# A two-layer hybrid diffusion block on one core: 768 tokens as 384 + 384 instead of 512 + 256

## The chip, the core and the metric

One core of a Trainium2 chip runs one program. The metric is device time in microseconds (us) of one execution; three runs of the kernel before gave a median of 2742.71 us (2742.32 to 2747.55). Engine names: PE (TensorE, the matmul array; its weight loads are shown apart as PEld), DVE (VectorE), ACT (ScalarE), POOL (GpSimd), SP (SyncE, which here only issues DMAs).

## The reference, cut to what matters

The input is 512 latent tokens `x` and 256 context tokens `ctx`, both of width 1024. Two layers each do a token-mixing sub-layer and an MLP:

```python
for l in range(2):
    h  = modulate(rms_norm(x,  g1), sh1,  sc1)      # latents: modulated by c
    hc = modulate(rms_norm(xc, g1), sh1c, sc1c)     # context: modulated by c_ctx
    # one input projection w_in for both: attention q,k,v; GLA q,k,v,gate; low-rank decay; two branch gates
    attn = window_attention(q, k, v, kc, vc, sink)  # blocks of 128; neighbours + all context keys
    o    = bidir_gla(...)                           # gated linear attention, starts from the context's states
    x = x + gt1 * ((sig_a * (attn @ w_branch_attn) + sig_b * (o @ w_branch_gla)) @ w_out)
    x = x + gt2 * (square(relu(modulate(rms_norm(x, g2), sh2, sc2) @ w_ff1)) @ w_ff2)
    # layer 0 does the same for xc with its own modulation; layer 1 needs of xc only keys, values and states
```

So the first layer works on 768 tokens in nearly every product, the second on 512 (and on 768 for keys, values and the GLA keys).

## The kernel before

Activations lie feature-major: features on the 128 partitions, tokens in the free dimension. One buffer of 768 columns holds the latents in columns 0 to 511 and the context in columns 512 to 767. `LAT` and `CTXS` are these two column ranges; six tiles of 128 tokens are numbered 0 to 3 (latents) and 4, 5 (context).

To reach float32 accuracy, each operand is kept as the exact sum of two fp32r parts, and each product is made of three matmuls for each 128 features of depth (`fm`, lines 172 to 174): weight-high by data-high, weight-high by data-low, weight-low by data-high. The weights are the stationary operand, so one matmul streams as many columns as there are tokens in the range: 512 for `LAT`, 256 for `CTXS`. `tm` (lines 184 to 186) makes token-major products, always 256 wide. A weight panel is loaded by SP, its high part made by ACT, its low part by DVE or POOL (`unit`).

A planner orders the instructions of each engine by a simulated time line, starting from the order in which the program emits them; work is thus interleaved across the emitted order. Each engine then runs its queue in order. PSUM banks for products are two called `mm` and, outside attention, one called `mx`; `t2` is a ring of six SBUF buffers for short-lived values.

The stages of the first layer and where the token ranges show:

- `norm(x, t0, n, ...)` normalises and modulates n tokens: four squares on ACT, three adds on DVE, a product with ones on PE, then for each of eight feature tiles one or two DVE operations, one ACT operation and sometimes one on POOL. It is called for at most 256 tokens at a time. A `late` call is emitted only when there is other work ahead of it.
- `keys`: key and value products by tile in the order 4, 5, 0, 1, 2, 3, with `late()` ahead of tile 0: it normalises tokens 256 to 511, tokens 0 to 255 having been normalised before.
- `attention`: blocks `[LAT, CTXS]`, group of heads by group of heads; gates and the branch projection of one block are spread over the steps of the other as PE filler.
- `gla`: low-rank input, decay, GLA queries and keys, gates, and the branch projection, by `LAT` and `CTXS`.
- `merge`: loads the parts of both branches, multiplies, adds and splits them into `Y`, by `LAT` and `CTXS`; the last two gates are made here.
- `project_out`: two parts, `[(512,256), (0,256)]` and `[(256,256)]`; after the first part its tokens are normalised for the MLP.
- `mlp`: eight chunks of 512 hidden features. Chunk 0's first product goes by the three ranges of 256, with `late` ahead of the second; chunks 1 to 7 by `whole = [(0,512), (512,256)]`; the second product by `whole` except in the last chunk, which goes part by part, each part being normalised for layer 1 when it is done (`done`), the last one late, inside `keys`.

In layer 1 the products over the latents are 512 wide; its groups are `[(0,256)]` and `[(256,256)]`.

Of the kernel before, what the change touches and what calls it, by code (L numbers as in the profile page):

```python
# [10 lines left out]
F32 = mybir.dt.float32  # L11
# [29 lines left out]
class Stream:  # L41
    """Columns off..off+T of the residual and of what is made of it."""
# [8 lines left out]


class Pair:
    """A tensor as the exact sum of two float32r parts."""
# [5 lines left out]
class Net:  # L60
# [13 lines left out]
    def shift(self, **bufs):  # L74
        """PSUM for the next phase: tiles by tag."""
# [42 lines left out]
    def wide(self, shape, dt, name):  # L118
        """One of the two places for [128, KD, TOK]."""
# [5 lines left out]
    def mm(self):  # L125
        """A bank for a product; every third one the extra bank if that is free."""
# [13 lines left out]
    def split(self, dst, src, idx, lo_eng=None):  # L140
        """dst.hi[idx] + dst.lo[idx] = src, exactly."""
# [15 lines left out]
    def panel(self, w, c0, rows=(0, D), lo_eng=None):  # L157
        """Columns c0..c0+256 of w: units of 512 rows."""
# [6 lines left out]
    def fm(self, ps, us, f, X, n, t0=0):  # L165
        """ps[:, :n] = (columns f of the units)^T X[.., t0:t0+n]."""
# [9 lines left out]
    def tm(self, ps, us, X, t):  # L176
        """ps = (tokens of tile t of X)^T panel."""
# [11 lines left out]
    def setup(self):  # L189
# [10 lines left out]
        # conditioning: silu of c and c_ctx as columns  # L200
# [13 lines left out]
        # thirty columns of zeros beside the two, so that a product fills its 32 partitions  # L214
# [18 lines left out]
    def layer_small(self, l):  # L233
        """Per-layer vectors as columns, and rows over all partitions."""
# [24 lines left out]
        # all powers of two: the ones' 1 / D is undone, and queries carry the attention scale  # L259
# [7 lines left out]
    def mod_group(self, l, m, bank):  # L267
        """One of the six modulation vectors of a layer, for both streams; summed in a bank or, without one, in SBUF."""
# [33 lines left out]
    def scales(self, x, t0, n):  # L302
        """1 / RMS of tokens t0..t0+n of x, over all partitions."""
# [37 lines left out]
    def attn_consts(self, pool, l):  # L341
        """Masks, and rotary tables with the gains in them."""
# [10 lines left out]
    def qk_norm(self, pool, ps, q, t):  # L353
        """RMS over each head, gain, rotation (latents): [128 tokens, 4 heads, 64]."""
# [744 lines left out]
```

## Time and profile before

| | |
|---|---|
| median of three runs | 2742.71 us |
| profiled execution, first to last instruction (span) | 2738.5 us |
| outside the span, against the median | 4.2 us |
| PE busy | 2612.3 us, 95% |
| DVE busy | 1456.3 us, 53% |
| ACT busy | 1097.8 us, 40% |
| POOL busy | 592.6 us, 22% |
| mean granted PE clock | 0.981 |

The profiled execution's own total is not given apart from its span; the 4.2 us are the difference between the median of the runs and the span. A busy PE is not PE at its peak: the length of a matmul in the trace includes its way through the array, and consecutive ones overlap. The pace is read from the starts: the distance from one start to the next.

### The profile page before, as it was taken

The numbers are of one execution on the slowest core, as the hardware profiler recorded it, in microseconds if no ns is written. First come the engines' busy times: TensorE is split into PE (matmuls) and PEld (weight loads), VectorE is DVE, ScalarE is ACT, GpSimd is POOL, SyncE is SP. The second block draws the span as 40 slices with busy tenths as digits, with TensorE's granted clock in tenths as the row PEclk, the third lists the DMA queues.
The fourth block names the chain that finished last, engine by engine and source line by source line (L and its number), as shares of the span: only waits on it lengthen the run. The fifth ranks groups of instructions, "written<-read, shape, count | busy, mean of one in ns | idle before, by whom it ended". The sixth has DMA issues, their size and how long they took to land. (4 is left out here: it accounts for less than half of the span.)

```text
span 2738.5 us, 41811 instructions
## 1 busy us (share of the span) xinstructions
PE 2612.3 (95%) x16891; PEld 2245.1 (82%) x16891; DVE 1456.3 (53%) x2779; ACT 1097.8 (40%) x2336; POOL 592.6 (22%) x396
## 2 busy tenths in 40 slices
PE   7899999999999899999999998899999998899999
PEld 4788887888888788888887897788788887878888
DVE  4666777534444566333333456777654446643443
ACT  3456554435252334222221244655355434423232
POOL 1313221211120212011111134332122112122122
PEclk7999999999999999999999999999999999999999
DMA  7213123233343533333434241222313325332333
GB/s 246 74 36 72 45 49 103 85 101 93 106 134 93 162 112 94 93 116 116 123 108 126 75 140 49 66 65 60 102 47 93 93 77 174 119 108 89 103 93 101
DMA packets 223830, 269.72 MB, mean 98 GB/s; under 512 B 18480, under 2 KB 185684, under 8 KB 223508
## 3 DMA queue, kind: packets, MB, share of 16 engines
q1 hardware_dynamic: 223636, 267.05, 32.5%
q8 instruction: 132, 2.16, 0.3%
q14 instruction: 62, 0.51, 0.1%
HBM read 244.21 MB, written 22.81 MB: 98 GB/s over the span
## 5 line engine op out<-in xcount | busy, mean ns | idle before, releaser
L97 ACT ACTIVATE whi<-raw 128x1024 fp32r<-128x1024 f32 x322 | 340.1, 1058 | 678.4 <-PE mm L173 270.0
L100 POOL TENSOR_TENSOR wlo<-raw,whi 128x1024 fp32r<-128x1024 f32 x132 | 319.1, 2425 | 926.3 <-ACT whi L97 846.2
L172 PE MATMUL mm<-H,whi 128*128 128x512 f32 (+1 forms) x1168 | 415.6, 356 | 5.8 <-ACT r L97 3.3
L173 PE MATMUL mm<-H,whi 128*128 128x512 f32 (+1 forms) x1168 | 410.8, 352 | 0.8 <-DVE H L337 0.7
L174 PE MATMUL mm<-H,wlo 128*128 128x512 f32 (+1 forms) x1168 | 410.4, 352 | 0.0
L100 DVE TENSOR_TENSOR wlo<-raw,whi 128x1024 fp32r<-128x1024 f32 x190 | 236.8, 1247 | 190.7 <-ACT whi L97 182.7
L172 PEld LDWEIGHTS mm<-H,whi 128*128 128x128 f32 x1168 | 223.2, 191 | 40.6 <-ACT r L97 5.6
L174 PEld LDWEIGHTS mm<-H,wlo 128*128 128x128 f32 x1168 | 222.8, 191 | 28.9 <-issue 0.2
L173 PEld LDWEIGHTS mm<-H,whi 128*128 128x128 f32 x1168 | 222.8, 191 | 28.6 <-DVE H L337 1.0
L103 DVE TENSOR_TENSOR r<-r 128x512 f32<-128x512 f32 (+1 forms) x104 | 89.3, 859 | 253.0 <-ACT hid L97 252.8
L172 PE MATMUL mm<-hid,whi 128*128 128x512 f32 (+1 forms) x552 | 187.8, 345 | 0.0
L173 PE MATMUL mm<-hid,whi 128*128 128x512 f32 (+1 forms) x552 | 186.2, 338 | 1.2 <-DVE hid L100 1.2
L174 PE MATMUL mm<-hid,wlo 128*128 128x512 f32 (+1 forms) x552 | 185.7, 337 | 0.0
L172 PE MATMUL mx<-H,whi 128*128 128x512 f32 (+1 forms) x496 | 171.0, 345 | 3.0 <-DVE sgr L842 2.7
L173 PE MATMUL mx<-H,whi 128*128 128x512 f32 (+1 forms) x496 | 170.2, 343 | 0.0
L174 PE MATMUL mx<-H,wlo 128*128 128x512 f32 (+1 forms) x496 | 168.9, 340 | 0.0
L958 DVE SCALAR_TENSOR_TENSOR x<-mm,mod,x 128x256 f32<-128x256 f32 (+1 forms) x138 | 84.4, 617 | 148.3 <-PE mm L174 148.3
L97 ACT ACTIVATE p<-p,nm 128x512 f32<-128x512 f32 (+1 forms) x128 | 98.1, 768 | 71.3 <-DVE nm L456 71.3
L172 PEld LDWEIGHTS mm<-hid,whi 128*128 128x128 f32 x552 | 104.4, 189 | 23.4 <-issue 8.6
L453 DVE CUSTOM_DVE_ANT_0 p<-S,mask 128x512 f32<-128x512 f32 (+1 forms) x128 | 96.4, 753 | 48.8 <-PE S L451 47.2
L173 PEld LDWEIGHTS mm<-hid,whi 128*128 128x128 f32 x552 | 104.4, 189 | 13.8 <-DVE hid L100 1.4
L174 PEld LDWEIGHTS mm<-hid,wlo 128*128 128x128 f32 x552 | 104.5, 189 | 11.5
(257 smaller groups left out, 6378.1 us busy)
## 6 DMA issues: line engine op xcount, KB each, us to landing
raw<-in_w_ff SPq DMA_DIRECT2D x136, 512.0 KB
raw<-in_w_mod SPq DMA_DIRECT2D x96, 512.0 KB
raw<-in_w_in SPq DMA_DIRECT2D x88, 512.0 KB
raw<-in_w_branch_attn SPq DMA_DIRECT2D x64, 256.0 KB
raw<-in_w_out SPq DMA_DIRECT2D x32, 512.0 KB
raw<-in_w_in SPq DMA_DIRECT2D x32, 256.0 KB
ya<-yd SPq DMA_DIRECT2D x32, 256.0 KB
raw<-in_w_branch_gla SPq DMA_DIRECT2D x16, 512.0 KB
```

What stands on the lines that cost most here:

```text
L97: return self.nc.scalar.activation(out=out, in_=in_, func=func, **kw)
L100: (eng or self.nc.vector).tensor_tensor(out=out, in0=a, in1=b, op=ALU.subtract)
L103: (eng or self.nc.vector).tensor_tensor(out=out, in0=a, in1=b, op=ALU.mult)
L172: nc.tensor.matmul(ps[:, :n], lhsT=wh, rhs=xh, start=(i == 0), stop=False)
L173: nc.tensor.matmul(ps[:, :n], lhsT=wh, rhs=xl, start=False, stop=False)
L174: nc.tensor.matmul(ps[:, :n], lhsT=wl, rhs=xh, start=False, stop=(i == len(ks) - 1))
L453: nc.vector.tensor_tensor_reduce(out=p[:, :nk], in0=S[:, s0:s0 + nk], in1=mask, scale=1.0, scalar=-3e38, op0=ALU.add, op1=ALU.max, accum_o ...
L958: nc.vector.scalar_tensor_tensor(out=xx, in0=ps[:, :n], scalar=self.mod2[:, 5, j, c:c + 1], in1=xx, op0=ALU.mult, op1=ALU.add)
```

## The change

The first layer's 768 columns are cut at 384 instead of 512. `HALVES` holds columns 384 to 767 (latent tile 3 and both context tiles) and columns 0 to 383 (latent tiles 0 to 2), in this order. All feature-major products over 768 tokens, the attention blocks and the parts of `project_out` and `mlp` go by these two; the scan and the read-out of the linear attention keep the split by latents and context (`streams`). Where the modulation differs between latents and context, a range is cut again at column 512 (`pieces`, `onto`, `norms`), so the first half is normalised as 128 + 256 tokens and the second as 256 + 128. `keys` goes by the tiles 4, 5, 3, 0, 1, 2. Layer 1's GLA keys and low-rank input are also made by halves; all else in layer 1 is as before. Comments and docstrings that the diff also removes are left out here.

```diff
+HALVES = [Stream(TOK // 2, TOK // 2, None), Stream(TOK // 2, 0, None)]
+def pieces(t0, n):
+    cut = min(max(SEQ, t0), t0 + n)
+    return [(a, b - a) for a, b in ((t0, cut), (cut, t0 + n)) if b > a]
...
+    def norms(self, x, t0, n, which, H):
+        for a, m in pieces(t0, n):
+            for b in range(a, a + m, 256):
+                self.norm(x, b, min(256, a + m - b), which, H)
...
     def keys(self, pool, H, us, uv, kT, v, late):
-        for t in CTXS.tiles + LAT.tiles:
+        for t in CTXS.tiles + LAT.tiles[-1:] + LAT.tiles[:-1]:
             if t == LAT.tiles[0]:
                 late()
...
+    def onto(self, x, ps, j, t0, n, gates):
+        for a, m in pieces(t0, n):
+            c, xx = int(a >= SEQ), x[:, j, a:a + m]
+            self.nc.vector.scalar_tensor_tensor(out=xx, in0=ps[:, a - t0:a - t0 + m], scalar=gates[:, j, c:c + 1],
+                                                in1=xx, op0=ALU.mult, op1=ALU.add)
     def project_out(self, Y, l, x, groups, done):
...
                     for t0, n in part:
-                        c = int(t0 >= SEQ)
-                        xx = x[:, j, t0:t0 + n]
                         ps = self.mm()
                         self.fm(ps, us, f, Y, n, t0)
-                        nc.vector.scalar_tensor_tensor(out=xx, in0=ps[:, :n], scalar=self.mod[:, 2, j, c:c + 1],
-                                                       in1=xx, op0=ALU.mult, op1=ALU.add)
+                        self.onto(x, ps, j, t0, n, self.mod[:, 2])
...
     def gla_low(self, pool, H, l):
-        for st in (CTXS, LAT):
+        for st in HALVES:
...
     def gla_project(self, pool, H, l, hd, sts):
...
-        for st in (CTXS, LAT):
-            tt = slice(st.off, st.off + st.T)
+        for st in HALVES:
             ps = self.mm()
             self.fm(ps, us, 1, H, st.T, st.off)
-            self.copy(ks[:, tt], ps[:, :st.T], self.either())
+            self.copy(ks[:, st.off:st.off + st.T], ps[:, :st.T], self.either())
             self.tick()
-            if st in sts:
-                ps = self.mm()
-                self.fm(ps, us, 0, H, st.T, st.off)
-                self.act(qs[:, tt], ps[:, :st.T], ACTF.Copy, scale=128.0 ** -0.5)
-                self.tick()
+        for st in sts:
+            ps = self.mm()
+            self.fm(ps, us, 0, H, st.T, st.off)
+            self.act(qs[:, st.off:st.off + st.T], ps[:, :st.T], ACTF.Copy, scale=128.0 ** -0.5)
+            self.tick()
...
-    def gla(self, pool, H, l, E, yb, sts):
+    def gla(self, pool, H, l, E, yb, sts, streams):
...
-            sg = {}
+            sg = [pool.tile([128, width], F32, name="sgr", tag=f"sgr{f}", bufs=1) for f in range(2)]
...
-            blocks = [LAT, CTXS] if CTXS in sts else [Stream(256, 0, 0), Stream(256, 256, 0)]
+            blocks = sts if CTXS in streams else [Stream(256, 0, 0), Stream(256, 256, 0)]
...
-        whole = [(0, SEQ)] + ([(SEQ, CTX)] if width > SEQ else [])
+        whole = [(s.off, s.T) for s in HALVES] if width > SEQ else [(0, SEQ)]
...
     def run(self, es):
-        self.norm(x, 0, 256, 1, H)
-        late = partial(self.norm, x, 256, 256, 1, H)
+        self.norms(x, TOK // 2, SEQ - TOK // 2, 1, H)
+        late = partial(self.norms, x, 0, TOK // 2, 1, H)
         for l in range(DEPTH):
-            sts = [LAT] if last else [LAT, CTXS]
-            groups = [[(0, 256)], [(256, 256)]] if last else [[(SEQ, CTX), (0, 256)], [(256, 256)]]
+            sts, streams = ([LAT], [LAT]) if last else (HALVES, [LAT, CTXS])
+            groups = [[(0, 256)], [(256, 256)]] if last else [[(s.off, s.T)] for s in HALVES]
```

## Rows read from the trace of the kernel before

**Rows 1.** The head of the profile's page: the span, and busy time, share and instructions of each engine with its number of instructions.

```profile
span 2738.5 us, 41811 instructions
PE 2612.3 (95%) x16891; PEld 2245.1 (82%) x16891; DVE 1456.3 (53%) x2779; ACT 1097.8 (40%) x2336; POOL 592.6 (22%) x396
```

**Rows 2.** Busy time by stage; a row is one stretch: its bounds and length in us, busy time of each engine with its instructions, granted PE clock, busy share of the DMA engines, GB/s. In order: keys of layer 0, its attention, its linear attention, its merge and the start of the output projection, the end of its MLP's chunk 0, its MLP's steady part, keys of layer 1, attention of layer 1, the steady part of layer 1's MLP.

```profile
57.00:104.00 47.00, 36.30 (x273) 33.32 (x272) 36.52 (x70) 25.92 (x60) 23.56 (x18) 0.96 0.37 128
104.00:480.00 376.00, 360.69 (x2776) 311.58 (x2776) 256.91 (x687) 198.63 (x541) 82.96 (x54) 0.99 0.22 57
480.00:930.00 450.00, 432.30 (x2743) 370.31 (x2743) 202.77 (x365) 178.84 (x425) 82.97 (x80) 0.99 0.35 106
930.00:1000.00 70.00, 61.90 (x419) 57.25 (x419) 44.87 (x60) 23.49 (x39) 21.09 (x16) 0.93 0.45 140
1058.00:1085.00 27.00, 23.66 (x165) 22.18 (x167) 17.28 (x35) 12.49 (x27) 11.84 (x6) 0.94 0.20 61
1150.00:1560.00 410.00, 410.00 (x2450) 334.02 (x2449) 148.05 (x215) 88.26 (x127) 53.63 (x22) 1.00 0.37 113
1634.00:1690.00 56.00, 46.16 (x348) 42.97 (x348) 47.13 (x84) 30.52 (x68) 25.29 (x19) 0.94 0.31 90
1690.00:1970.00 280.00, 261.34 (x2107) 228.96 (x2106) 201.46 (x525) 151.94 (x377) 77.35 (x46) 0.97 0.26 66
```

**Rows 3.** The time line of PE in the MLP of layer 0: start in us, length in us, engine, line, operation, output and inputs, shape. First the last 256-wide matmuls of a run and the start of a 512-wide run, then the far end of the same run.

```profile
1369.06 0.28 PE L174 MATMUL mm<-H,wlo 128*128 128x256 f32 x1
...
1369.42 0.28 PE L174 MATMUL mm<-H,wlo 128*128 128x256 f32 x1
1369.54 0.40 PE L172 MATMUL mm<-H,whi 128*128 128x512 f32 x1
...
1370.70 0.39 PE L174 MATMUL mm<-H,wlo 128*128 128x512 f32 x1
...
1373.42 0.39 PE L174 MATMUL mm<-H,wlo 128*128 128x512 f32 x1
```

**Rows 4.** The time line of PE in attention of layer 0, four places where two 384-wide score matmuls (one row, x2) stand between other fp32r matmuls; the row behind each tells where they end.

```profile
217.36 0.52 PE L448 MATMUL S<-kT,qT 128*128 128x384 f32 x2
217.72 0.40 PE L451 MATMUL S<-kT,qT 128*128 128x256 f32 x2
229.05 0.51 PE L448 MATMUL S<-kT,qT 128*128 128x384 f32 x2
229.40 0.40 PE L451 MATMUL S<-kT,qT 128*128 128x256 f32 x2
308.17 0.52 PE L448 MATMUL S<-kT,qT 128*128 128x384 f32 x2
308.52 0.40 PE L451 MATMUL S<-kT,qT 128*128 128x256 f32 x2
422.59 0.50 PE L448 MATMUL S<-kT,qT 128*128 128x384 f32 x2
422.93 0.39 PE L451 MATMUL S<-kT,qT 128*128 128x256 f32 x2
```

**Rows 5.** Who PE waited for, by stage: engine, tile and line that waited, who released it, us in total, times, longest. The first two rows are of 930 to 1000 us, the next of 1058 to 1085, the next two of 57 to 104, the next three of 1634 to 1690, the last of 104 to 480.

```profile
PE mm L173 <- DVE Y L100: 7.3, 5, 3.2
PE mx L172 <- ACT sg L97: 0.7, 1, 0.7
PE mm L172 <- ACT r L97: 3.3, 1, 3.3
PE pt L395 <- ACT kd L97: 6.0, 2, 5.8
PE mm L184 <- DVE xn L103: 1.6, 2, 1.3
PE pt L395 <- ACT kd L97: 3.7, 2, 2.4
PE pt L395 <- DVE kd L100: 2.3, 3, 1.1
PE mx L186 <- DVE H L337: 1.3, 1, 1.3
PE S L448 <- DVE rmax L453: 6.7, 8, 2.0
```

**Rows 6.** The late normalisation of tokens 256 to 511 in chunk 0 of layer 0's MLP, DVE's operations of 1049 to 1067 us by kind: line, operation, tiles, shape, number, busy us, mean ns of one, idle time before them and who ended it.

```profile
L330 DVE SCALAR_TENSOR_TENSOR xr<-x,A,rs 128x256 f32<-128x256 f32 x8 | 3.9, 539 | 5.0 <-ACT rs L97 4.3 <-POOL H L100 0.6
L337 DVE SCALAR_TENSOR_TENSOR H<-xr,mod,H 128x256 fp32r<-128x256 f32 x5 | 2.3, 481 | 0.0
L106 DVE TENSOR_TENSOR acc<-acc,sq 128x512 f32<-128x512 f32 x3 | 2.1, 691 | 1.5 <-ACT sq L97 1.4
L332 DVE TENSOR_SCALAR xr<-xr,mod 128x256 f32<-128x256 f32 x3 | 1.0, 347 | 0.0
```

**Rows 7.** The time lines of ACT and DVE around the same call, its first square and its last high and low parts of `H`; and of PE, the last matmul before its wait and the first behind it.

```profile
1049.37 0.62 ACT L97 ACTIVATE acc<-x 128x512 f32<-128x512 f32 x1
1065.42 0.48 DVE L337 SCALAR_TENSOR_TENSOR H<-xr,mod,H 128x256 fp32r<-128x256 f32 x1
1058.27 0.28 PE L174 MATMUL mm<-H,wlo 128*128 128x256 f32 x1
1061.89 0.38 PE L172 MATMUL mm<-H,whi 128*128 128x256 f32 x1 [3.34 <-ACT r L97]
```

**Rows 8.** Groups of DVE instructions of the whole kernel by shape, columns as in rows 6: the same addition to `x` at 512 and at 256 columns, and an addition at 256.

```profile
L958 DVE SCALAR_TENSOR_TENSOR x<-mm,mod,x 128x512 f32<-128x512 f32 x70 | 51.8, 749 | 98.5 <-PE mm L174 98.5
L958 DVE SCALAR_TENSOR_TENSOR x<-mm,mod,x 128x256 f32<-128x256 f32 x68 | 32.7, 482 | 49.8 <-PE mm L174 49.8
L106 DVE TENSOR_TENSOR ya<-mm,ya 128x256 f32<-128x256 f32 x72 | 29.1, 419 | 13.7 <-PE mm L174 13.5
```

More of the change, by code (lines that the diff above doesn't have):

```diff
@@ L805, in gla_read @@
             self.split(G, o, (slice(None), f, slice(st.off, st.off + st.T)), nc.gpsimd)
-    def gla(self, pool, H, l, E, yb, sts):
+    def gla(self, pool, H, l, E, yb, sts, streams):
         nc = self.nc
+        width = sum(st.T for st in sts)
         w = self.io["w_in"][l]
@@ L828, in gla @@
             for st in (CTXS, LAT):
-                S[st], prev = self.gla_scan(st, pool, Eh, ends[st], qs, ks, v, prev, st in sts)
+                S[st], prev = self.gla_scan(st, pool, Eh, ends[st], qs, ks, v, prev, st in streams)
             for _ in fill:
@@ L839, in gla @@
                     self.fm(ps, us, f, H, st.T, st.off)
-                    s = pool.tile([128, st.T], F32, name="sgr", tag=f"sgr{st.col}{f}", bufs=1)
+                    s = sg[f][:, st.off:st.off + st.T]
                     self.sigmoid(s, ps[:, :st.T])
@@ L843, in gla @@
                                                    op0=ALU.mult, op1=ALU.mult)
-                    sg[st, f] = s
-            G = self.pair(pool, [2, sts[-1].off + sts[-1].T], "G")
-            for st in sts:
-                self.gla_read(st, pool, Eh, S[st], v, [sg[st, f] for f in range(2)], G)
+            G = self.pair(pool, [2, width], "G")
+            for st in streams:
+                self.gla_read(st, pool, Eh, S[st], v, [g[:, st.off:st.off + st.T] for g in sg], G)
             for _ in self.gate(H, l, O_SA, 2 * hd, 2, sts, use):
@@ L851, in gla, with mix @@
         return fill
-    def mix(self, l, x, H, us, uv, sts, late):
+    def mix(self, l, x, H, us, uv, sts, streams, late):
         tc, io = self.tc, self.io
@@ L869, in mix @@
             for j in range(KD):
-                n = sts[-1].off + sts[-1].T
+                n = sum(st.T for st in sts)
                 self.nc.sync.dma_start(out=self.yd[:, j, :n], in_=ya[:, j, :n])
@@ L877, in mix @@
                 self.bg = self.mods(0, (2, 3, 4, 5), None)
-            fill = self.gla(pool, H, l, E, yb, sts)
+            fill = self.gla(pool, H, l, E, yb, sts, streams)
             for _ in fill:
@@ L1004, in run @@
             self.load_x(pool, x, LAT, self.io["x"])
-        self.norm(x, 0, 256, 1, H)
-        late = partial(self.norm, x, 256, 256, 1, H)
+        self.norms(x, TOK // 2, SEQ - TOK // 2, 1, H)
+        late = partial(self.norms, x, 0, TOK // 2, 1, H)
         for l in range(DEPTH):
             last = l == DEPTH - 1
-            sts = [LAT] if last else [LAT, CTXS]
-            groups = [[(0, 256)], [(256, 256)]] if last else [[(SEQ, CTX), (0, 256)], [(256, 256)]]
-            yb = self.mix(l, x, H, us, uv, sts, late)
+            sts, streams = ([LAT], [LAT]) if last else (HALVES, [LAT, CTXS])
+            groups = [[(0, 256)], [(256, 256)]] if last else [[(s.off, s.T)] for s in HALVES]
+            yb = self.mix(l, x, H, us, uv, sts, streams, late)
             with tc.tile_pool(name="yp", bufs=1, reuse_waits="tile") as yp:
@@ L1042, in done @@
                             us, uv = [self.panel(self.io["w_in"][l + 1], o) for o in (O_K, O_V)]
-                        late = partial(self.norm, x, t0, n, 1, H)
+                        late = partial(self.norms, x, t0, n, 1, H)
                         if part is groups[0]:
```

9 lines of the change are left out of this document (3 added, 6 removed).

## The prediction

> **What bounds the kernel now.** Read the page's head first: PE is busy 95% of the span and no other engine above 53% [rows 1]. A busy PE proves little, so go to the stages. In the steady part of the first layer's MLP, PE is busy all 410 us at a granted clock of 1.00, with DVE at 36% and ACT at 22% [rows 2]: there the time is the number of matmuls times their pace. In attention DVE is busy 257 of 376 us and PE has short waits for the score maxima. Only at the joints between stages does PE stand: 57 to 104 us and 1634 to 1690 (keys, DVE busy 37 of 47 and 47 of 56), 930 to 1000 (merge, clock 0.93), 1058 to 1085 (late normalisation, clock 0.94). The waits of these joints are small: 7.3 us for `Y` in the merge, 3.3 in the MLP's chunk 0, and in the keys mostly for the last tile's own chain (6.0 and 3.7 for `kd`) [rows 5]. So two questions decide: what 384 columns cost on PE against 512 and 256, and what the new cut does to the joints.
>
> **The pace.** Starts tell it [rows 3]. Three steps of 256-wide matmuls take 1369.42 - 1369.06 = 0.36 us, 120.0 ns each. Twelve steps far inside a 512-wide run take 1373.42 - 1370.70 = 2.72 us, 226.7 ns each. The difference of 106.7 ns for 256 columns is 0.4167 ns a column, and both leave the same constant: 13.3 ns a matmul. On this line a 384-wide one takes 173.3 ns, and two take 346.7 ns, the same as 226.7 + 120.0.
>
> By `fm` and the loops, the products that had two ranges and still have two are, in pairs of matmuls: low-rank input 24, sixteen gates 384, GLA queries and keys 192, GLA gates 192, the two branches 192 each, first MLP product without chunk 0 28 x 24 = 672, second without the last chunk 56 x 12 = 672; together 2520 pairs. On the line they change nothing.
>
> Is 384 on the line? The only 384-wide rows are scores, between other shapes [rows 4]: two of them take 0.36, 0.35, 0.35 and 0.34 us, 175.0 ns each on the mean, with 10 ns of rounding on every start. Bounds, for the 5040 + 768 matmuls that become 384 wide: at 175.0 ns, 5808 x 1.7 = 9.9 us lost; at the smallest, 170 ns, 19 us gained; the largest, 180 ns, would lose 39 us, but a single row carries 5 ns of rounding. I take the line: score matmuls stand just behind a change of width, which costs something itself, as the next term shows.
>
> **Fewer matmuls.** Where three ranges of 256 become two of 384, the columns stay and a constant goes. `project_out` in layer 0: 8 feature tiles x 24 = 192 matmuls fewer. Chunk 0's first product: 4 x 24 = 96. The last chunk's second product: 8 x 12 = 96. Together 384 x 13.3 ns = **5.1 us gained**. The Trainium skill (TensorE: Matmul & The Clock Gate, section Back-to-back issue gap) gives a constant of about 2.5 ns at full clock instead; by it these 384 would save 1.0 us and the sum below would be 2737 us. The trace disagrees with it here, 13.3 ns at both widths, and I go by the trace.
>
> **No change of width.** The first five steps of a 512-wide run behind a 256-wide one take 1370.70 - 1369.54 = 1.16 us, 232 ns each, 27 ns more in all than five later ones [rows 3]. The first layer has 181 products of 512 columns by the loops (1 + 16 + 8 + 8 + 32 + 32 + 28 + 56), each at most once behind a narrower one: 181 x 27 = 4.8 us at the most. The planner puts some 512-wide ones behind each other, so I take **3.5 us gained**; zero if equal widths have a start-up of their own.
>
> **The merge.** The first part of `project_out` now needs only columns 384 to 767 of `Y`, and three open banks hold 3 x 24 x 173.3 = 12.5 us of work instead of 3 x 24 x 120 = 8.6. PE can go on for 3.8 us more before it depends on the last of `Y`. It waits 7.3 us there and the clock falls to 0.93 over 70 us, about 5 us lost [rows 2, 5]. DVE's work there stays (two 384-wide operations for 512 + 256). I take **3 us gained**; bounds 0 and 12.
>
> **The normalisations.** Three sets of 768 tokens (for attention in layer 0, for its MLP, for layer 1) become 128 + 256 and 256 + 128 instead of three of 256. DVE spends 3.9 + 2.3 + 2.1 + 1.0 = 9.3 us on one of 256 [rows 6]. One of 128 is not in the trace: halving an operation from 512 to 256 columns takes it from 749 to 482 ns [rows 8], so 267 ns go and 128 columns should take about 348, 0.72 of 256; the three adds fall from 691 to 419. That is (3.9 + 2.3 + 1.0) x 0.72 + 1.3 = 6.5 us. A set costs 2 x 9.3 + 2 x 6.5 - 3 x 9.3 = 3.7 us of DVE more. What lies around each set:
>
> In `keys` of layer 0 DVE is nearly the bound, and the first latent tile needed is now tile 3, whose input comes in last: **2 us lost**, bounds 0 and 6. In chunk 0 of the MLP the first half is normalised behind 8 x 24 x 173.3 = 33 us of PE work instead of 23, but the late half is 384 tokens behind 4 x 24 x 173.3 = 16.6 us instead of 256 tokens behind 23.0: **1 us lost**, bounds 3 gained (the wait of rows 5 gone) and 13 lost (rival below). In `keys` of layer 1 the same shift happens; the first half is normalised behind 8 x 12 x 173.3 = 16.6 us instead of 11.5, the late one behind three tiles instead of four: **1 us gained**, bounds 4 and -6.
>
> **The rest costs nothing, by this cover.** The addition to `x` is cut once more (128 + 256 and 384 for 512 + 256): about 0.2 us more on DVE, 8 x 7 times, 12 us in an MLP where DVE is idle 64% [rows 2]; without that cover it would be those 12 us. Panels, their high and low parts and the weight DMAs stay in number. The context's scan needs the first half's GLA keys alone, which still come first. Transfers of `yd` and `gd` change only in width, 384 instead of 512 and 256. In attention the latent steps had (12288 + 18432) / 8 = 3840 columns of filler each and the context steps 24576 / 4 = 6144; now the first block's six steps have 6144 and the second's six have 3072, 30720 over the eight latent steps either way. The score waits are 6.7 us in all [rows 5], so I put this at nothing, within 4 us either way.
>
> **The sum.** -5.1 - 3.5 - 3 + 2 + 1 - 1 = -9.6 us. The profiled span of 2738.5 becomes 2728.9; with the 4.2 us by which the median lies above that span, the forecast is **2733 us**. One run of this kernel can be told from no change at about 0.2%, 5.5 us.
>
> **Rivals.**
> A: the 384-wide matmul has the pace of the score rows, 175.0 ns. Then 9.9 us come back and the time is 2743 us: no change. For it: these are the only rows of that width. Against it: their neighbours differ in width, and both known widths lie on one line.
> B, slower: the late normalisation outgrows its cover. In chunk 0 the late 256 tokens took from 1049.37 to 1065.90, 16.5 us, and PE, with 23.0 us of cover, still waited 3.3 [rows 5, 7]: the call started about 9.8 us into the cover. If it starts as late again and 6.5 us for 128 tokens come behind, 9.8 + 16.5 + 6.5 - 16.6 = 16.2 us of wait, 13 more than now. With half as much in each of the two keys stages, 26 us are lost against 9.6 gained: 2759 us. It decides from 15 us of added wait on. For it: the call is still emitted behind the first half's products, and `t2` has six buffers. Against it: before, the start was late because the preceding normalisation was itself squeezed into 23 us of PE work; it now has 33.
> C: the joints gain more: the merge's wait and its low clock go wholly (12 us instead of 3) and the keys of layer 1 gain 4: 2721 us. For it: the first part needs half of `Y`. Against it: DVE makes `Y` feature tile by feature tile, so the last tile is late for both halves.
>
> **Chances.** The forecast, 2727 to 2737: 0.43. A and what else ends within 5.5 us of no change: 0.26. B: 0.18. C: 0.13. Faster by over 0.2% is the forecast and C, 0.56; the same 0.26; slower 0.18. The range goes from C's time to short of B's full price, 2721 to 2753 us.
>
> **What would show it.** PE should have 384 fewer fp32r matmuls, about 16,500 in all; 384-wide starts 173 ns apart with no start-up of a run; in the MLP's steady part the same length as before, less about 2 us; the wait for `Y` in the merge under 5 us; the waits for `H` behind chunk 0's first half and behind tile 3 of the keys under 5 us each. A pace of 175 ns or more, or waits for `H` of 10 us and more at any of the three normalisations, would make the forecast wrong.

## The result and the profile after

The changed kernel takes 2780.8 us (median of four runs, 2774.1 to 2785.1) beside 2742.5 us of the kernel before on the same chip (2741.9 to 2747.6): ratio 1.013, interval 1.0116 to 1.0145. It is 38 us slower; 2733 us were forecast, 2721 to 2753. Its profiled run has a span of 2781.8 us, 43.3 more than [rows 1].

The head of the page after:

```profile
span 2781.8 us, 41265 instructions
PE 2615.1 (94%) x16519; PEld 2348.2 (84%) x16519; DVE 1471.9 (53%) x2884; ACT 1108.3 (40%) x2370; POOL 591.0 (21%) x405
```

PE has 372 matmul records fewer than in [rows 1] (384 by the loops; a few records can be missing) and is no longer busy for it: the 43 us are idle time and low clock (PE is idle 166.7 us of the span, before 126.2). Where? Cut both traces at the first matmul of each stage (first key product, first query product, first product with the decay's inputs, first `Y`, last `Y`, first `hid`, last `hid` of the layer, and so on):

| stage, length in us | before | after | difference |
|---|---|---|---|
| keys of layer 0 | 61.2 | 71.3 | +10.0 |
| attention, then GLA and merge of layer 0 | 378.7, 468.8 | 381.2, 469.7 | +2.4, +0.9 |
| output projection of layer 0 | 84.2 | 76.2 | -8.0 |
| chunk 0 of layer 0's MLP, up to its second product | 41.3 | 53.9 | +12.6 |
| rest of that MLP | 555.9 | 552.2 | -3.7 |
| keys of layer 1 | 55.4 | 68.7 | +13.2 |
| attention, GLA and merge of layer 1 | 619.2 | 632.7 | +13.5 |
| output projection and MLP of layer 1 | 53.3, 369.7 | 54.1, 369.9 | +0.8, +0.2 |

(1.2 us more lie ahead of the first key product; parts carry one rounding.) So four stages lose 49 us and two gain 12. Busy time by stage after, columns as in [rows 2]: keys of layer 0, its output projection, chunk 0, the rest of the MLP, keys of layer 1, its attention and GLA; and the 22 us in the middle of chunk 0 alone.

```profile
44.70:116.00 71.30, 53.24 (x371) 47.82 (x369) 53.85 (x111) 38.26 (x92) 27.69 (x24) 0.88 0.40 132
966.90:1043.10 76.20, 71.22 (x394) 68.87 (x393) 59.02 (x97) 34.86 (x61) 18.87 (x15) 0.98 0.44 138
1043.10:1097.00 53.90, 38.67 (x211) 36.62 (x210) 28.18 (x55) 22.07 (x46) 12.80 (x10) 0.84 0.16 49
1097.00:1649.20 552.20, 552.20 (x3276) 510.03 (x3274) 215.58 (x372) 131.25 (x199) 83.33 (x37) 1.00 0.35 109
1649.20:1717.90 68.70, 51.84 (x351) 48.40 (x349) 47.21 (x94) 32.43 (x75) 25.90 (x21) 0.84 0.25 78
1717.90:2350.60 632.70, 599.48 (x3963) 526.69 (x3961) 374.14 (x807) 307.28 (x711) 146.19 (x106) 0.98 0.28 81
1060.00:1082.00 22.00, 6.77 (x27) 4.96 (x27) 14.87 (x39) 11.60 (x29) 5.32 (x5) 0.61 0.07 24
```

The rest of the MLP is pure PE, 552.20 of 552.20 us at a clock of 1.00. Chunk 0 and both keys stages have PE idle a quarter of the time, and the clock falls with it. In the 22 us of the last row no engine is full: PE 6.8, DVE 14.9, ACT 11.6. That is a chain of waits, not an engine at its limit.

What the chain is shows the time line of ACT and DVE in chunk 0 (start, length, what; in brackets the engine's idle time before it): the last addition to the late half's `x`, the relus of the first half's four products, the first squares of the two pieces of the late normalisation, the second piece's logarithm, and the last operation on ACT.

```profile
1043.44 0.62 DVE L627 SCALAR_TENSOR_TENSOR x<-mm,mod,x 128x384 f32<-128x384 f32 x1
...
1048.53 0.49 ACT L105 ACTIVATE r<-mm 128x384 f32<-128x384 f32 x1 [4.20 <-PE mm L182]
1051.76 0.49 ACT L105 ACTIVATE r<-mx 128x384 f32<-128x384 f32 x1 [2.18 <-PE mx L182]
1055.92 0.49 ACT L105 ACTIVATE r<-mm 128x384 f32<-128x384 f32 x1 [3.11 <-PE mm L182]
1060.09 0.49 ACT L105 ACTIVATE r<-mm 128x384 f32<-128x384 f32 x1 [3.11 <-PE mm L182]
1060.47 0.62 ACT L105 ACTIVATE acc<-x 128x512 f32<-128x512 f32 x1
...
1070.79 0.42 ACT L105 ACTIVATE acc<-x 128x256 f32<-128x256 f32 x1 [0.37 <-DVE H L350]
...
1077.09 0.37 ACT L105 ACTIVATE rs<-pt,eps 128x128 f32<-128x128 f32 x1 [2.12 <-PE pt L322]
...
1082.16 0.29 ACT L105 ACTIVATE H<-xr 128x128 fp32r<-128x128 f32 x1
```

`x` is complete at 1044.06 us. ACT idles 12.6 us in four gaps until 1060, but the first square comes at 1060.47, directly behind the fourth relu: the call stands behind the first half's four products in emitted order, and so in ACT's queue. From there the chain of both pieces takes until 1082.45, 22.0 us. (DVE ends its last operation 0.2 us later.) The second piece's squares (1070.79) come only when the first piece is largely applied: the first two of them wait for operations on `H`, which by the code free the six buffers of `t2`. PE's waits in chunk 0 (who waited, for whom: us in all, times, longest):

```profile
PE pt L322 <- DVE acc L114: 13.6, 2, 9.9
PE mx L180 <- ACT H L105: 1.6, 1, 1.6
```

The first row is PE in front of the matmuls with ones of the two pieces, waiting for sums of squares. In the two keys stages the same two kinds appear smaller, and behind them a wait for the last keys, the first row of layer 0, the second of layer 1 (before: 6.0 and 3.7, [rows 5]):

```profile
PE pt L408 <- ACT kd L105: 9.4, 2, 5.9
...
PE pt L408 <- ACT kd L105: 7.7, 2, 7.3
```

The GLA of layer 1 is another matter. Its code for the 512-wide latents is untouched, yet it has waits that the kernel before does not have there (before, nothing at all for `sgr`, `a` or `st`):

```profile
PE mx L180 <- DVE sgr L859: 4.0, 3, 3.5
PE pt L809 <- DVE a L805: 2.2, 2, 1.2
PE pt L809 <- DVE st L768: 2.0, 1, 2.0
```

The first is a wait for the extra bank `mx`; that the other two follow from it is tested below. `mm()` gives every third product this bank by a counter. The first layer calls it 20 times less (8 in `project_out`, 4 in chunk 0, 8 in the last chunk), so the counter stands at 523 instead of 543 when layer 1's GLA heads start: remainder 1 instead of 0. From there on both kernels call it equally often, so all heads keep the shift.

Two theories share the 38 us, then, each with a rival. **O, the order**: the late normalisation is emitted behind all the work that could hide it. Its rival **A, the amount**: 384 tokens in two pieces are longer than 16.6 us of products wherever they start. And **P, the phase** of the bank counter, against the rival that the GLA only inherits what came before it.

### The profile page after: what moved, and what is told of

Same layout as the page of the kernel before. It is cut to its first block, busy times and chain, and to the rows that moved or that the text cites. A ratio compares the mean times of both kernels' runs of the same rounds, so it can differ in the third digit from the quotient of the medians.

```text
span 2781.8 us, 41265 instructions
## 1 busy us (share of the span) xinstructions
PE 2615.1 (94%) x16519; PEld 2348.2 (84%) x16519; DVE 1471.9 (53%) x2884; ACT 1108.3 (40%) x2370; POOL 591.0 (21%) x405
## 5 line engine op out<-in xcount | busy, mean ns | idle before, releaser
L180 PE MATMUL mm<-H,whi 128*128 128x384 f32 (+2 forms) x1072 | 378.5, 354 | 3.2 <-DVE sgr L859 3.2
L181 PE MATMUL mm<-H,whi 128*128 128x384 f32 (+2 forms) x1072 | 375.6, 350 | 0.0
L182 PE MATMUL mm<-H,wlo 128*128 128x384 f32 (+2 forms) x1072 | 374.7, 350 | 0.1
L180 PE MATMUL mx<-H,whi 128*128 128x384 f32 (+2 forms) x560 | 198.0, 354 | 8.9 <-DVE sgr L859 5.0
L180 PE MATMUL mm<-hid,whi 128*128 128x384 f32 (+2 forms) x564 | 197.9, 356 | 0.1
L181 PE MATMUL mm<-hid,whi 128*128 128x384 f32 (+2 forms) x564 | 194.9, 348 | 3.0 <-DVE hid L108 3.0
L181 PE MATMUL mx<-H,whi 128*128 128x384 f32 (+2 forms) x560 | 196.5, 351 | 0.8 <-DVE H L350 0.7
L182 PE MATMUL mx<-H,wlo 128*128 128x384 f32 (+2 forms) x560 | 196.4, 351 | 0.0
L182 PE MATMUL mm<-hid,wlo 128*128 128x384 f32 (+2 forms) x564 | 194.7, 348 | 0.0
L627 DVE SCALAR_TENSOR_TENSOR x<-mm,mod,x 128x256 f32<-128x256 f32 (+3 forms) x210 | 107.9, 537 | 157.9 <-PE mm L182 157.9
L180 PEld LDWEIGHTS mx<-H,whi 128*128 128x128 f32 x560 | 106.5, 190 | 19.0 <-DVE sgr L859 6.4
L192 PE MATMUL mm<-whi,H 128*128 128x256 f32 x384 | 112.5, 294 | 7.6 <-ACT H L105 6.3
L498 PE MATMUL pt<-pT,v 128*64 128x128 f32 x1280 | 105.4, 287 | 9.7 <-DVE pT L120 6.3
```

The lines of the kernel that those rows point to most:

```text
L180: nc.tensor.matmul(ps[:, :n], lhsT=wh, rhs=xh, start=(i == 0), stop=False)
L181: nc.tensor.matmul(ps[:, :n], lhsT=wh, rhs=xl, start=False, stop=False)
L182: nc.tensor.matmul(ps[:, :n], lhsT=wl, rhs=xh, start=False, stop=(i == len(ks) - 1))
L192: nc.tensor.matmul(ps, lhsT=xh, rhs=u.hi[:, k], start=(i == 0), stop=False)
L498: nc.tensor.matmul(po[h * 64:(h + 1) * 64, 0:128], lhsT=v[:, keys[i + a], g * HD:(g + 1) * HD], rhs=pT[:, (2 * a + h) * 128:(2 * a + h + 1 ...
L627: self.nc.vector.scalar_tensor_tensor(out=xx, in0=ps[:, a - t0:a - t0 + m], scalar=gates[:, j, c:c + 1], in1=xx, op0=ALU.mult, op1=ALU.add)
```

## The experiments

Lengths by stage in us, from the profiled run of each (single executions; most runs of one kernel lie within 5 us of their median, single ones 9 off it, so a microsecond or two of a stage says little; the run of e6 in the table is the longest of its ten, that of e1 the shortest of its four).

| | before | after | e1 | e2 | e3 | e6 | e8 | e11 | e13 | e14 |
|---|---|---|---|---|---|---|---|---|---|---|
| keys 0 | 61.2 | 71.3 | 67.4 | 70.6 | 61.2 | 67.2 | 65.3 | 63.7 | 66.6 | 70.4 |
| projection 0 | 84.2 | 76.2 | 76.2 | 75.8 | 80.8 | 76.3 | 75.9 | 75.6 | 75.8 | 75.7 |
| chunk 0 | 41.3 | 53.9 | 46.3 | 54.0 | 41.4 | 46.9 | 50.4 | 39.7 | 49.8 | 46.2 |
| rest of MLP 0 | 555.9 | 552.2 | 552.2 | 552.2 | 554.1 | 552.2 | 552.2 | 553.1 | 553.1 | 553.1 |
| keys 1 | 55.4 | 68.7 | 57.5 | 67.3 | 54.5 | 56.2 | 63.6 | 51.9 | 59.0 | 59.3 |
| attention, GLA 1 | 619.2 | 632.7 | 633.2 | 620.8 | 620.7 | 625.5 | 620.9 | 619.3 | 632.5 | 635.7 |
| MLP 1 | 369.7 | 369.9 | 370.0 | 370.1 | 372.7 | 361.0 | 364.6 | 363.4 | 369.8 | 365.4 |

### Is it the joints or the steady parts? (e3)

From the changed kernel, only the joints are put back:

```diff
-        for t in CTXS.tiles + LAT.tiles[-1:] + LAT.tiles[:-1]:
+        for t in CTXS.tiles + LAT.tiles:
...
-        self.norms(x, TOK // 2, SEQ - TOK // 2, 1, H)
-        late = partial(self.norms, x, 0, TOK // 2, 1, H)
+        self.norm(x, 0, 256, 1, H)
+        late = partial(self.norm, x, 256, 256, 1, H)
...
-            groups = [[(0, 256)], [(256, 256)]] if last else [[(s.off, s.T)] for s in HALVES]
+            groups = [[(0, 256)], [(256, 256)]] if last else [[(SEQ, CTX), (0, 256)], [(256, 256)]]
```

> The changed kernel, with 384 + 384 kept in the products of the steady parts (low-rank input, gates, GLA queries and keys, branches, MLP's first product without chunk 0 by its own order of parts) and in the attention blocks, but the joints as before: project_out, chunk 0 and the last chunk in three parts of 256, normalisations of 256, keys in the old order. Theories O and A alike: the whole loss lies in the joints (and the phase of the extra bank, which is the old one here): 2739 us, the kernel before less some 3.5 us for products that no longer change width. Rival W: the two parts of 384 cost in the steady products or the attention blocks themselves: 2755 us or more.

Measured: 2741.7 us, the kernel before beside it 2745.4; ratio 0.9991, interval 0.9981 to 1.0001. The whole loss is in the joints and the phase; rival W falls. What 384 + 384 brings in the steady parts alone cannot be told from nothing by the total; the rest of the MLP shows 1.8 us. There PE never waits and the length hardly scatters: 552.2 us in after, e1, e2, e6 and e8, 555.9 or 556.0 in before, e7, e9, e10 and e12.

### The late call first (e1)

In `keys` of both layers and in chunk 0 of layer 0's MLP:

```diff
-            if t == LAT.tiles[0]:
+            if t == CTXS.tiles[0]:
                 late()
...
-                        if (t0, n) == halves[1]:
+                        if (t0, n) == halves[0 if width > SEQ else 1]:
                             late()
```

> The changed kernel (2780.8 us) with the late half's normalisation emitted ahead of the first half's products instead of behind the available ones: in keys of both layers at the first tile instead of the fourth, in chunk 0 of layer 0's MLP ahead of both halves. All work stays. Theory O (order): in the changed kernel the late squares stand in ACT's queue behind the four relus of the first half though x is ready 16 us earlier, and PE then waits. About 25 us come back: 8 of the 10 us that keys of layer 0 lost, 10 of 12.6 in chunk 0, 8 of 13 in keys of layer 1: 2756 us, and PE waits of 10.4 us (chunk 0) and 7.5 us (keys of layer 1) shrink under 3 us. Rival A (amount): 384 tokens in two pieces are too much DVE and ACT work for this cover wherever they start, since the first half's chain then waits for the late one: under 6 us come back, 2775 us or more.

Measured: 2761.8 us, ratio 1.0065 (1.0049 to 1.0082); 18 to 19 us come back, half of the loss. By stage 7.6 in chunk 0, 11.2 in keys of layer 1, but 3.9 of 10 in keys of layer 0. The order counts, and it is not all: chunk 0 keeps 5 us. PE's waits in chunk 0 now:

```profile
PE pt L322 <- DVE acc L114: 4.3, 1, 4.3
PE mm L180 <- ACT r L105: 3.9, 1, 3.9
```

The relus now stand behind the normalisation in ACT's queue. Three products of the first half run and fill the three open banks; PE stands at the second piece's matmul with ones, and then the fourth product waits on for a bank, until the first relu behind the normalisation frees one:

```profile
1056.95 0.49 ACT L105 ACTIVATE r<-mm 128x384 f32<-128x384 f32 x1 [0.21 <-DVE H L350]
```
```profile
1057.50 0.69 PE L180 MATMUL mm<-H,whi 128*128 128x384 f32 x1 [3.94 <-ACT r L105]
```

The stage of layer 1's attention and GLA stays long (633.2 us), so its loss does not come in with the late normalisation. (The 10.4 us of the expectation are 9.9 in the trace.)

### The phase of the extra bank (e2, e9)

Both add one statement at the start of the heads; e2 to the changed kernel, e9, with `(1 - self.turn) % 3`, to the kernel before:

```diff
         ga = self.gla_low(pool, H, l)
+        if l == 1:
+            self.turn += -self.turn % 3
```

> The changed kernel with one more line: at the start of layer 1's GLA heads the turn that sends every third product to the extra PSUM bank is brought to a multiple of three, as it stands there in the kernel before (543; in the changed kernel 523). Layer 1's GLA is 13 us longer in the changed kernel though its code is the same. Theory P (phase): the gate product now lies in the extra bank that the decay also wants, and the bank waits for VectorE's multiply; 8 to 13 us come back, 2768 to 2773 us. Rival: the loss comes in with what enters the stage (the late norm, the order of loads); nothing comes back, within 3 us of 2780.8.

> The kernel before with the turn brought to one modulo three at the start of layer 1's GLA heads, where the changed kernel has it; nothing of the change itself. Theory P: the phase alone costs it 8 to 13 us in layer 1's GLA, 2753 to 2758 us, with waits of the extra bank for VectorE's multiply with the gate. Rival: the phase only hurts together with the 384-wide low-rank input and keys of the changed kernel; the same as before.

Measured: e2 2769.1 us, ratio 1.0091 (1.0076 to 1.0107) where the changed kernel had 1.013, 11 to 12 us less, nearly all of it in layer 1's attention and GLA (620.8, before 619.2). e9 2755.5 us, ratio 1.0037 (1.0025 to 1.0050), 10.8 us more than before; its attention and GLA of layer 1 are 12.6 us longer, and it has the same waits as the changed kernel:

```profile
PE mx L172 <- DVE sgr L844: 4.1, 3, 3.5
PE pt L793 <- DVE st L752: 2.2, 1, 2.2
PE pt L793 <- DVE a L789: 2.1, 2, 1.2
```

P is shown from both sides: taken out of the changed kernel, all but 1.6 us of this stage's loss and all three waits go; put alone into the kernel before, they come. In the trace of the changed kernel one of these waits can be followed: a gate's product lies in `mx`, the next head's key product takes `mx` too, and starts at 2162.62 us, behind DVE's multiply of the gate:

```profile
2161.82 0.75 DVE L859 SCALAR_TENSOR_TENSOR sgr<-mx,lcol,sgr 128x512 f32<-128x512 f32 x1 [0.79 <-ACT sgr L105]
```
```profile
2162.62 0.44 PE L180 MATMUL mx<-H,whi 128*128 128x384 f32 x1 [3.45 <-DVE sgr L859]
```

### Both corrections (e6)

e1 and e2 together, the late call first also in layer 1's chunk 0 (`halves[0]` in both layers).

> The changed kernel with both corrections, the late normalisation ahead everywhere (also in chunk 0 of layer 1's MLP, where PE waits 7 us in both kernels) and the turn at a multiple of three at layer 1's GLA. O and P: 25 + 10 us come back and 4 more in layer 1's MLP: about 2742 us, the kernel before. If O or P falls, 2755 us or more.

Measured: 2736.1 us, ratio 0.9966 (0.9954 to 0.9978): faster than the kernel before, and 6 us better than expected. Layer 1's MLP gives 8.9 us instead of 4; the other joints are as in e1. Layer 1's attention and GLA show 625.5 us in this longest of its runs, e2 620.8. 5.6 us in chunk 0 and 6 in keys of layer 0 stay.

### What is left: PE's queue, or the length? (e8, e13, e14)

e8 is e6 with the late call one product group later: `t == CTXS.tiles[1]` in keys, between the two panels of the first half in chunk 0.

> The changed kernel with the turn set as in the run with both corrections, but the late normalisation emitted one product group later: in keys behind the first tile, in chunk 0 behind the first two of four products. Ahead of everything, its matmul with ones stands before the first half's products in PE's queue, and PE waited 4.6 + 4.3 us for it at the start of chunk 0 and 3.3 us in keys of layer 0 with products ready behind it. Theory Q (what is left of the loss in the joints is PE's own queue): those waits go, 5 us back in chunk 0 and 3 in keys of layer 0 against the run with both corrections, 2728 us. Rival A (what is left is the amount of 384 tokens in two pieces): the waits only move, 2734 us or more.

Measured: 2750.1 us, ratio 1.0018 (1.0008 to 1.0027), 14 us worse than e6. Theory Q falls. Chunk 0 grows by 3.5 us and keys of layer 1 by 7.4. In chunk 0 PE now waits once, longer:

```profile
PE pt L322 <- DVE acc L114: 8.9, 1, 8.9
```

It is the second piece's matmul with ones, but nothing that was ready stands behind it: the four products of the first half are through at 1052, and the next product needs the late half's `H`. The chain only starts later than in e6, behind the second relu and 9.1 us into the stage:

```profile
1043.69 0.62 ACT L105 ACTIVATE acc<-x 128x512 f32<-128x512 f32 x1
```

Nor was PE's queue what e6 lost in chunk 0: it has the same two waits as e1 (4.3 us for the sums, 3.9 for a relu), and the second, for the relu's bank, would have held the fourth product without the first. So the call in one piece keeps the relus waiting if it is emitted first, and starts late if it is emitted later.

So the call was cut in two emitted steps: `stat` (squares and additions of both pieces) and the rest (ones, logarithm, application). e13 emits both at the old place, so that the second piece's squares no longer follow the first piece's application; e14 emits `stat` first and the rest at the old place. In e13, e14 and e11 the first half's two pieces, normalised for layer 1 in the last chunk, get the new order too.

```diff
+    def two(self, x, t0, n, which, H):
+        cut = [(b, min(256, a + m - b)) for a, m in pieces(t0, n) for b in range(a, a + m, 256)]
+        accs = [self.stat(x, b, m) for b, m in cut]
+        yield
+        for (b, m), acc in zip(cut, accs):
+            self.norm(x, b, m, which, H, self.rms(acc, m))
```

> The changed kernel with one edit: where the late normalisation stands, the squares and additions of both pieces come ahead of the first piece's application. In the changed kernel the second piece's squares wait for buffers of the first's application, and its matmul with ones keeps PE 10.4 us in chunk 0. Theory S: the 22.0 us from the first square to the last H become about 17: 5 us back in chunk 0 and 3 in each of the two keys stages, 2770 us against 2781. Rival: ACT and VectorE are busy through the 22 us and only the order within changes: within 3 us of the changed kernel.

> The changed kernel with one edit: the squares and additions of both late pieces are emitted ahead of the first half's products, the matmuls with ones and the application stay behind them, where they were. Theory S: the statistics (8.7 us in chunk 0 for the first piece, and the second piece's) leave the exposed stretch; of 22.0 us about 13 stay: 9 us back in chunk 0, 5 in keys of layer 0, 6 in keys of layer 1, 2761 us. Rival: the exposed stretch is set by the application alone: under 4 us back in all, 2777 us.

Measured: e13 2762.4 us, ratio 1.0066 (1.005 to 1.0082), 18 us back with the order of a few ACT and DVE instructions alone; 4.1 in chunk 0 where 5 were expected, 4.7 in keys of layer 0 and 9.7 in keys of layer 1 where 3 each were. How much of the 9.7 comes from the first half's new order was not told apart. The time line of ACT in its chunk 0:

```profile
1052.04 0.62 ACT L105 ACTIVATE acc<-x 128x512 f32<-128x512 f32 x1
1052.56 1.66 ACT L105 ACTIVATE sq<-x 128x512 f32<-128x512 f32 x3
1054.12 0.40 ACT L105 ACTIVATE acc<-x 128x256 f32<-128x256 f32 x1
...
1069.58 0.40 ACT L105 ACTIVATE H<-xr,mod 128x128 fp32r<-128x128 f32 x1 [0.72 <-DVE xr L357]
```

The chain takes 1069.98 - 1052.04 = 17.9 us instead of 22.0. e14: 2759.9 us, ratio 1.0055 (1.0037 to 1.0073). Chunk 0 gives 7.7 us, keys of layer 1 9.4, keys of layer 0 only 0.9 of the 5 expected; against e13 it wins 3.6 us in chunk 0 and 4.4 in layer 1's MLP and loses 3.8 in keys of layer 0. Its only wait in chunk 0 is for the application:

```profile
PE mx L180 <- ACT H L105: 7.7, 1, 7.7
```

### Statistics first, the rest behind one product (e11, e12)

e11 is the changed kernel with the phase of e2, `stat` ahead of the first product and the rest behind the first of four products (keys: behind the first tile). e12 is the kernel before with the same two steps, its late part one piece.

```diff
+                    late = late()
+                    next(late)
                     for t0, n in halves:
-                        if (t0, n) == halves[1]:
-                            late()
...
                                 ff1(us[p], p, f, t0, n)
+                                list(late)
```

> The changed kernel with the turn at a multiple of three and the normalisation in two emitted steps: the squares and additions of both late pieces ahead of the first product, the rest (matmul with ones, logarithm, application) behind the first of the four products in chunk 0 and behind the first tile in keys. So ACT's squares stand ahead of the relus, and PE has work in front of the matmuls with ones. Theory S (three queues in series: the squares behind relus on ACT, the second piece's squares behind the first piece's application by the buffers of t2, the matmuls with ones ahead of ready products on PE): chunk 0 takes 43 us (run with both corrections: 46.9), keys of layer 0 64 (67.2), keys of layer 1 55 (56.2): 2728 us, faster than before. Rival L (length: 384 tokens in two pieces take 22 us from the first square to the last H, against 16.6 us of products, whatever the order): 2735 us or more, the run with both corrections.

> The kernel before with the same two steps at the same places; its late part is one piece of 256. Theory S: the squares no longer stand behind relus and PE has work ahead of the ones: chunk 0 of layer 0 within 2 us of 41, chunk 0 of layer 1 8 us shorter, keys the same within 2 us: 2736 us. Beside the run of the changed kernel in this form it tells what the change is worth when neither waits in a queue: 8 us less for the changed one by the terms that held; within 4 us if the 384-token normalisation eats them.

Measured: e11 2729.4 us, ratio 0.9936 (0.9915 to 0.9957), 15 us faster than the kernel before. Chunk 0 takes 39.7 us, less than before (41.3), keys of layer 1 51.9 (55.4), keys of layer 0 63.7 (61.2). L, the length, falls. S holds for the two queues on ACT (squares behind relus, second piece behind first); that the matmuls with ones held up ready products in chunk 0 no run shows. The time line of ACT in its chunk 0: the second piece's squares, the first relu behind them, the two logarithms, the next relu.

```profile
1041.59 1.02 ACT L105 ACTIVATE sq<-x 128x256 f32<-128x256 f32 x3
1044.46 0.49 ACT L105 ACTIVATE r<-mm 128x384 f32<-128x384 f32 x1 [1.86 <-PE mm L182]
...
1047.24 0.47 ACT L105 ACTIVATE rs<-pt,eps 128x256 f32<-128x256 f32 x1 [1.72 <-PE pt L329]
...
1052.07 0.37 ACT L105 ACTIVATE rs<-pt,eps 128x128 f32<-128x128 f32 x1 [0.43 <-DVE H L364]
...
1059.41 0.49 ACT L105 ACTIVATE r<-mx 128x384 f32<-128x384 f32 x1
```

All squares end at 1042.6, two microseconds ahead of the first relu. The second relu waits until 1059.41 behind the application, but PE goes on: three open banks take three products of 384 columns, 3 x 24 x 173.3 = 12.5 us, and it waits once:

```profile
PE mx L180 <- ACT r L105: 2.5, 1, 2.5
```

e12: 2747.0 us, ratio 1.0012 (1.0003 to 1.0022); 2736 was expected. Layer 1's MLP gives 7.7 us back as expected, but chunk 0 of layer 0 takes 46.5 us (41.3) and keys of layer 1 57.9 (55.4). In its chunk 0 the relus stand behind the application as in e11, but here three banks hold only 3 x 24 x 120.0 = 8.6 us of 256-wide products:

```profile
PE mm L172 <- ACT r L97: 7.2, 2, 5.0
```

What the change is worth with this order is therefore not 8 but 18 us (2747.0 - 2729.4). That part of it is the order, which suits two wide parts better than three narrow ones, is a reading of these waits (7.2 us for relus against 2.5), not a run of its own.

### The late call moved in the kernel before (e7, e10)

e7 has e6's places in the kernel before, e10 those of e8, both without the split.

> The kernel before with the late normalisation emitted ahead of the first product, in keys and in chunk 0 of both layers' MLPs. Here the late part is 256 tokens in one piece, with more product work behind it in the first layer. Theory O: the old place costs the old kernel too, but only where two equal parts remain, as in layer 1's MLP: 8 us back there, as the changed kernel with the same edit showed, and up to 3.5 in chunk 0 of layer 0 (its wait there); keys stay within 3 us. About 2733 us, 0.996 of before. Rival: the order matters only for 384 tokens; the same as before within 0.2%.

> The kernel before with the late normalisation emitted behind the first tile in keys and behind the first two products in chunk 0 of both layers. Beside the changed kernel with the same place it tells what the change itself is worth once the order is right in both: by the terms that held (384 fewer matmuls 5.1 us, no change of width 3.5, the joint of the projection 8, less one more piece of normalisation) the changed one should be 6 to 12 us shorter. If the change is worth nothing once the order is right, the two are within 4 us. This kernel itself: 2732 us, no more than 3 us from the one with the late normalisation first.

Measured: e7 2748.5 us, ratio 1.0009 (0.9998 to 1.0020); e10 2745.6 us, ratio 1.0003 (0.9991 to 1.0015). Both as before, where 2732 to 2733 were expected. e7's layer 1 MLP is 8.6 us shorter (361.1), but its chunk 0 in layer 0 takes 48.2 us (41.3) and its keys of layer 1 60.1 (55.4): what one joint gains, the others lose. So the place of the call in the kernel before was no plain flaw; with three parts of 256 it fits. Against e10, e8 is 4 us longer, not 6 to 12 shorter: with the call in one piece in the middle the change costs 4 us. With the call first it is worth 12: e6 at 0.9966 of before against e7 at 1.0009.

## Why the prediction was wrong, step by step

**The pace: right.** The time line of PE in the MLP of layer 0 after, twenty-one steps of 384-wide matmuls apart:

```profile
1375.84 0.33 PE L182 MATMUL mm<-H,wlo 128*128 128x384 f32 x1
...
1379.48 0.33 PE L182 MATMUL mm<-H,wlo 128*128 128x384 f32 x1
```

3.64 / 21 = 173.3 ns, the 173.3 that were read off the line; rival A's 175.0 is out. At 0.4167 ns a column (granted clock 1.00, the level of 2.4 GHz) 384 columns take 160 ns, so the constant is again 13.3 ns. The Trainium skill's 2.5 ns, given for an isolated matmul (TensorE: Matmul & The Clock Gate, section Back-to-back issue gap), does not hold for these products at any of the three widths.

**Fewer matmuls, no change of width: right where PE never waits.** In the rest of layer 0's MLP 96 matmuls fewer are 1.3 us and 84 products without a change of width 84 x 27 = 2.3 us at the most, 3.6 together; the stage is 3.7 us shorter. e3, which keeps the 96, shows 1.8. In attention and GLA of layer 0 nothing of it is seen. Over all profiled runs GLA there is rather some 2.6 us longer with halves (nine runs, 467.9 to 472.4, mean 470.0) than with latents and context (five runs, 466.2 to 468.9, mean 467.4), and attention 1.4 (379.9 and 378.5 in the mean); why stays open.

**The merge: right, a little small.** The projection's stage is 8.0 us shorter; 192 matmuls are 2.6 of it, so 5.4 come from the wait and the clock, for which 3 were taken. The clock of the stage is 0.98, and the wait for `Y` is 3.8 us in all instead of 7.3.

**The late normalisation in chunk 0: this step failed.** The sum had +1; it is +12.6, nearly 14 with the 1.3 us of matmuls saved. The sum of the sizes came out: 16.5 + 6.5 = 23 us were worked out for 384 tokens, 22.0 came, and the cover was 16.6 us, the four products, as given. That is in part luck: the 256 tokens took 14 us, not 16.5 (in these ACT stood 4.8 for the matmul with ones, which came behind products on PE), and the 128 added 8, not 6.5. What was wrong is the start. The prediction let the call start early in its cover, because "before, the start was late because the preceding normalisation was itself squeezed". But [rows 7] already had the first square at 1049.37 us, and what stood directly ahead of it on ACT, in the kernel before, was the fourth relu of the first part:

```profile
1049.09 0.38 ACT L97 ACTIVATE r<-mm 128x256 f32<-128x256 f32 x1 [1.50 <-PE mm L174]
```

The call waited for its place in the queue. With three parts, four products were still to come behind that place; with two parts, none. It started 17.4 us into the stage (1060.47 against 1043.1), when the cover was used up. Rival B had the mechanism, and still took the start at 9.8 us, 7.6 too early. It had worked the 9.8 out from PE's wait of 3.3 us as if that were for `H`; [rows 7] shows it ended by a relu, and from the stage's start the call began 12.9 us in (1049.37 against 1036.5). Nor is the wait after the one for `H` that was named as a sign: PE stands 13.6 us for the sums of squares and 1.6 for `H`.

**Keys of both layers: the same step failed.** +2 and -1 were taken; +10.0 and +13.2 came. Order alone (e1, e13) gives back 3.9 and 4.7 us in layer 0 and 11.2 and 9.7 in layer 1; the new order of tiles was not tried by itself. The sum of these three stages' misses, 8.0 + 11.6 + 14.2, is 34 us.

**The phase of the bank counter: not seen at all.** "The rest costs nothing" went through panels, DMAs, scans and fillers, but not through a counter that runs on over both layers; this term stood at nothing without a reason. It costs 11 to 12 us in a stage whose 512-wide code was not changed.

These two are nearly the whole miss: 34 + 12 = 46 us of the 48 between forecast and result.

**How far the amount counts.** O alone was too simple as well. e1 and e6 leave 5 us in chunk 0 although the call starts as early as it can, and e7 and e8 show that an earlier or a later place can lose. What e11 shows is that the normalisation is not too long (39.7 us, under the kernel before) once its statistics stand ahead of the first product and the rest behind one product. Open is what still makes keys of layer 0 2.5 us longer than before in e11.

## What to carry to other kernels

When a change makes the parts of a loop fewer and wider, look at each call that is emitted between two parts: its cover is what stands behind it, and its start is its place in each engine's queue, read from the instruction directly ahead of its first one, not from when its data were ready. A call that uses several engines in turn takes a place in each of their queues; here it was worth more to emit its statistics ahead of the first product and the rest behind one product than to move it whole. And a counter that deals out banks over the whole program is part of the change: twenty products fewer here shifted which product met which bank two stages later.

## What the runs showed of the hardware that was not expected

A wait cost more than its own length. In the 22 us of chunk 0 in which PE was busy for 6.8, the mean granted clock was 0.61. From 1075 to 1079 us it was 0.50, the level of 1.2 GHz, after PE had idled 9.9 us; the 384-wide products behind the waits start 0.32 us apart instead of 0.173:

```profile
1080.55 0.53 PE L181 MATMUL mm<-H,whi 128*128 128x384 f32 x1
1080.87 0.53 PE L182 MATMUL mm<-H,wlo 128*128 128x384 f32 x1
1081.19 0.53 PE L181 MATMUL mm<-H,whi 128*128 128x384 f32 x1
```

From 1082.6 us to the end of the stage the clock is 1.00 again. In chunk 0 this is little: PE is busy for 38.7 us, before for 38.1 with 1.3 us more of matmuls, so some 2 of the 12.6 us, an estimate from the busy times. In keys of layer 1 it is more: PE is busy 51.8 us for 351 matmuls at a clock of 0.84, where the kernel before needs 45.6 for 347, some 6 of the 13.2 us. That stage in the kernel before, and then chunk 0 in e11, with all but 2.5 us of the waits gone:

```profile
1633.80:1689.20 55.40, 45.56 (x347) 42.24 (x346) 47.33 (x84) 30.33 (x68) 25.29 (x19) 0.95 0.30 89
1038.50:1078.30 39.80, 37.26 (x212) 36.43 (x211) 25.88 (x54) 20.40 (x44) 13.04 (x10) 0.96 0.22 68
```

The prediction counted the clock in the merge, but priced the waits of the normalisations, its rival B too, at their own length.
